# In a two-layer decoder trunk, two of the four token sums of the seven-product stage are prepared some slots later, and a weight splitter is held to one piece per slot

## The chip, the cores and the metric

The kernel runs on one core of one Trainium2 chip. The metric is the device time of one execution in microseconds (us). Before the change the median of three runs was 1451.13 us (1450.94 to 1451.14).

## What is computed

Two decoder layers on x of shape (1, 512, 1024) in float32. Layer 0 mixes tokens with dilated sliding-window attention, layer 1 with a recurrent block (RG-LRU). After either mixer comes the same gated ConvFFN, and every sub-layer is wrapped in two RMSNorms. The change sits in the ConvFFN alone, which runs once per layer:

```python
def conv_ffn(x, w_up, conv_w, conv_b, w_down):
    u = causal_dwconv(x @ w_up, conv_w, conv_b)      # w_up: 1024 x 6144, conv over 3 tokens
    g, v = u[..., :D_FF], u[..., D_FF:]              # D_FF = 3072
    return (jax.nn.gelu(g, approximate=True) * v) @ w_down

for layer in range(DEPTH):                           # DEPTH = 2
    x = x + rms_norm(mixer(rms_norm(x, ...)), ...)
    h = rms_norm(x, norm_ffn_pre[layer])
    h = conv_ffn(h, ffn_w_up[layer], ffn_conv_w[layer], ffn_conv_b[layer], ffn_w_down[layer])
    x = x + rms_norm(h, norm_ffn_post[layer])
```

## The kernel before

**Numbers in two parts.** Every float32 operand of a matmul is split into a high part (ScalarE, a copy rounded to fp32r, L153) and a low part (VectorE, the difference, L154). A product is then three matmul passes: high by high, high by low, low by high (`PASSES`). So each piece of weights also takes one ScalarE and one VectorE instruction. In the profile `whi` and `wlo` are the two parts of weights, `raw` the weights as loaded, `hT` the transposed activations (two parts), `T` the token sums, `B` their unsplit form, `ps` PSUM banks, `u` the convolved outputs.

**The queue of weight pieces.** `plan` lists the weight chunks in the order of their use. `load` (L274 on) brings a chunk into one of three `raw` buffers. `pump` (L245 on) takes the next piece of a chunk and writes its two parts into a pair of buffers. There are `HALVES = 16` such pairs, and `state["live"]` counts those in use: a piece adds one or two, `done` takes one or two off once the matmuls that read it have been written. `tick` (L303 on) runs between the parts of the program: it advances the side jobs (generators, which say after how many ticks they want to go on) and then lets `pump` split one piece when 12 (`HALVES - 4`) or more pairs are in use, two when fewer are.

**Seven products for eight.** For the FFN's column groups j = 3 to 10 (`SEVEN`) one of the two column tiles of each half of `w_up` is computed with a scheme of seven half-size products in place of eight (`seven`, `chain`). It needs sums of weight blocks, made in place in `raw` by VectorE (`across` L205, `upper` L209) and by adding DMAs on GpSimd's queue (`add_rows` L191), and sums of token blocks, made by the side job `token_sums` (L732 on): its `whole` adds the two parts of `hT` (L749), a subtraction follows (L764 to L780), and `parted` splits the sum into its home `T` (two ScalarE and two VectorE instructions). The third sum is made of `b12`, the fourth of `b21`.

**Slots.** The order of the stage is written out in slots. A cycle of 15 slots (`CYCLE`) holds one chain: its seven products stand at the slots of `AT` (`{5: 0, 1: 3, 3: 4, 2: 8, 6: 9, 7: 14, 4: 20}`, product: slot; 20 lies in the next cycle), and the slots between hold quarters of ordinary products (L340 matmuls). In the first cycle slot 5 is empty, since no chain came before. `slot` (L793 on) writes the slot's matmuls (L833 for a chain product, 12 of them), then what has come due of `later`, then calls `tick`. Of `later` three things matter here: after product 3 the `seed` (ScalarE: L843 saves one bank to `part`, L844 writes the negated bank `a` into bank `c`), after products 6 and 7 the subtractions L848 and L851, and after each finished tile the convolution (`finish`: ScalarE L679, VectorE L683 twice, then L695 or L697). Product 2 in slot 8 adds to the bank that the seed reads and product 6 in slot 9 to the one that it writes, so product 2 waits for the seed. The third token sum is read by product 7 (slot 14), the fourth by product 4 (slot 20).

Every engine works through its own instructions in the order in which they were written, so what stands ahead of the seed on ScalarE is set by which slot's `tick` wrote it. Pieces run about one cycle ahead: those that the first cycle splits are used in the second.

Of the kernel before, what the change touches and what calls it, by code (L numbers as in the profile page):

```python
# [32 lines left out]
HALVES = 16  # L33
# [45 lines left out]
def kernel(  # L79
# [38 lines left out]
    def nm(s):  # L118
        uid[0] += 1
        return f"{s}{uid[0]}"  # L120

    def gen(dt=F32, s="g"):
        return gp.tile([P, 512], dt, tag="g", name=nm(s))

    def psum(s="ps"):
        return pp.tile([P, 512], F32, tag="ps", name=nm(s))
# [25 lines left out]
    def split(hi, lo, raw):  # L152
        nc.scalar.activation(hi, raw, AF.Copy)  # L153
        nc.vector.tensor_tensor(lo, raw, hi.bitcast(F32), op=ALU.subtract)  # L154

    plan = []
    state = {"dma": 0, "cv": 0, "used": 0, "live": 0, "next": 0, "hold": False}
    raws, units, pieces = {}, {}, []
    sides, first_w, first_y, one = [], [], [], []

# [124 lines left out]
    def chunk():  # L285
        i = state["next"]
        state["next"] += 1
        return i

    def take(i, j):  # L290
        while (i, j) not in units:
            before = state["live"]
            pump(1)
            assert before != state["live"], (i, j, state)
        return units[i, j]

    def done(n=2):
        state["live"] -= n
# [4 lines left out]
    def tick():  # L303
        for s in list(sides):
            s[0] -= 1
            if s[0] <= 0:
                try:
                    s[0] = next(s[1])
                except StopIteration:
                    sides.remove(s)  # L310
        if not state["hold"]:
            pump(1 if state["live"] >= HALVES - 4 else 2)

    def drain():
        while sides:
            tick()
# [21 lines left out]
    def mm3(dst, l, r, start, stop):  # L338
        for n, (a, b) in enumerate(PASSES):
            mm(dst, l[a], r[b], start=start and n == 0, stop=stop and n == 2)  # L340
# [391 lines left out]
    def token_sums(hT, T):  # L732

        assert len(sides) == 1
        d = dp.tile([P, 4, D], F32, name=nm("x_kept"))
        nc.gpsimd.dma_start(d, X[0])
        kept.append(d)
        homes = cp.tile([P, 4, D], F32R, tag="x_sb", name=nm("T"))
        homes = [homes[:, n] for n in range(4)]
        homes += [cp.tile([P, D], F32R, tag="gain", name=nm("T"), bufs=2) for _ in range(2)]  # L740
        homes = [[h[:, 0:512], h[:, 512:1024]] for h in homes]
        homes += [[gen(F32R, "T") for _ in range(2)] for _ in range(2)]
        homes = [[h.rearrange("p (k t) -> p k t", k=2) for h in hs] for hs in homes]
        yield 1

        def both(k0, n):
            o = gen(s="B").rearrange("p (k t) -> p k t", k=2)
            hi, lo = (h[:, k0 : k0 + 2, n * 256 : n * 256 + 256] for h in hT)
            tt(o, hi.bitcast(F32), lo.bitcast(F32), op=ALU.add)  # L749
            return o  # L750

        tt = nc.vector.tensor_tensor

        def whole(k0, n):
            return [both(k0 + 2 * k, n) for k in range(2)]

        def parted(n, b):
            for k in range(2):
                split(homes[2 * n][k], homes[2 * n + 1][k], b[k])

        b11, b12 = whole(0, 0), whole(0, 1)
        yield 1
        for k in range(2):
            tt(b11[k], b11[k], b12[k], op=ALU.subtract)  # L764
        parted(0, b11)
        yield 1
        b22 = whole(4, 1)
        for k in range(2):
            tt(b12[k], b12[k], b22[k], op=ALU.subtract)
            tt(b22[k], b22[k], b11[k], op=ALU.add)  # L770
        yield 1
        parted(1, b22)
        T.extend([homes[2 * n], homes[2 * n + 1]] for n in range(4))
        yield 5
        parted(2, b12)
        yield 4
        b21 = whole(4, 0)
        yield 1
        for k in range(2):
            tt(b21[k], b21[k], b22[k], op=ALU.subtract)  # L780
        yield 1
        parted(3, b21)
# [3 lines left out]
    def seven(hT, T, begin, before):  # L786

        due = []

        def later(n, f):  # L790
            due.append([n, f])

        def slot(emit):  # L793
            emit()
            for d in list(due):
                d[0] -= 1
                if d[0] < 0:
                    due.remove(d)
                    d[1]()
            tick()  # L800

        def block(kr, n):
            return lambda h, k: hT[h][:, 4 * kr + k, n * 256 : n * 256 + 256]

        def turn(n):
            return lambda h, k: T[n][h][k // 2][:, k % 2]

        right = {
            1: block(0, 0), 2: block(1, 0), 3: block(1, 1), 5: turn(0), 6: turn(1), 7: turn(2), 4: turn(3),
        }  # L810

        def finish(b, ps, j):
            f = begin(b, ps, j)
            later(1, f)

        def chain(j, b0):
            i = chunk()
            y = {}
            t = []

            def step(n):
                name, b = LEFT[n]
                W = take(i, name)
                if b not in y:
                    y[b] = psum()
                if not t:
                    t.append(gen(s="part"))
                p5, z = t[0][:, 0:256], t[0][:, 256:512]
                a = y[0][:, 0:256] if 0 in y else None
                c = y[1][:, 0:256]  # L830
                for k in range(4):
                    for q, (wa, ha) in enumerate(PASSES):
                        mm(  # L833
                            y[b][:, 0:256], W[wa][0][:, k, :], right[n](ha, k), start=n in (1, 5) and k == q == 0,
                            stop=k == 3 and q == 2, skip_group_check=True,
                        )
                done(1)
                if n == 5:
                    later(1, lambda: nc.scalar.activation(p5, c, AF.Copy))
                elif n == 3:  # L840

                    def seed():
                        nc.scalar.activation(z, c, AF.Copy)  # L843
                        nc.scalar.activation(c, a, AF.Copy, scale=-1.0)  # L844

                    later(1, seed)
                elif n == 6:
                    later(1, lambda: nc.vector.tensor_tensor(y[0][:, 256:512], z, c, op=ALU.subtract))  # L848
                    later(2, lambda: finish(b0, y[0], j))
                elif n == 7:  # L850
                    later(1, lambda: nc.vector.tensor_tensor(y[1][:, 256:512], c, p5, op=ALU.subtract))  # L851
                elif n == 4:
                    later(1, lambda: finish(b0 + 1, y[1], j))

            return lambda n: lambda: step(n)

        def quarters(i, m, j, b):
            ps = []

            def quarter(n):  # L860
                W = take(i, m)
                if not n:
                    ps.append(psum())
                for k in (2 * n, 2 * n + 1):
                    mm3(
                        ps[0], [w[k // 4][:, k % 4, :] for w in W], [h[:, k, :] for h in hT], k == 0, k == KD - 1
                    )
                if n % 2:
                    done(1)
                if n == 3:  # L870
                    later(1, lambda: finish(b, ps[0], j))

            return [lambda n=n: quarter(n) for n in range(4)]

        steps = {}
        fill = quarters(before, 1, SEVEN[0] - 1, 3)
        for n, j in enumerate(SEVEN):
            f = chain(j, 0)
            steps.update((CYCLE * n + AT[p], f(p)) for p in AT)
            i = chunk()  # L880
            steps.update((CYCLE * n + m, q) for m, q in zip((1, 2, 6, 7, 10, 11, 12, 13), fill + quarters(i, 0, j, 2)))
            fill = quarters(i, 1, j, 3)
        after = chunk()
        end = CYCLE * len(SEVEN)
        steps[end + 3] = steps.pop(max(steps))
        fill += quarters(after, 0, SEVEN[-1] + 1, 0)
        for m in range(max(steps) + 1):
            if m in steps or m >= end:
                slot(steps[m] if m in steps else fill.pop(0))
        for f in fill:  # L890
            slot(f)
        while due:
            slot(lambda: None)
        return after

    def attention(hT, post, pre):
# [536 lines left out]
```

## Time and profile before

| what | value |
|---|---|
| median of three runs | 1451.13 us (1450.94 to 1451.14) |
| the profiled execution, own time | 1451.21 us |
| its span, first to last instruction | 1449.4 us |
| mean granted TensorE clock | 0.997 |
| VectorE busy | 970.3 us (67%) |
| ScalarE busy | 734.9 us (51%) |
| GpSimd busy | 177.6 us (12%) |

The profile shows one execution. "Busy" is the time in which an engine had an instruction in work; PE is TensorE's matmuls, PEld its weight loads, DVE is VectorE, ACT ScalarE, POOL GpSimd. A row of the timeline gives the start in us from the span's start, the duration in us of a run of like instructions, their number after the x, and in brackets how long the engine had been idle before and which instruction released it. The stage with the chains runs once in layer 0 (its first chain begins at 563.28 us) and once in layer 1 (1113.26 us).

### The profile page before, as it was taken

The numbers are of one execution on the slowest core, as the hardware profiler recorded it, in microseconds if no ns is written. First come the engines' busy times: TensorE is split into PE (matmuls) and PEld (weight loads), VectorE is DVE, ScalarE is ACT, GpSimd is POOL, SyncE is SP. The second block draws the span as 40 slices with busy tenths as digits, with TensorE's granted clock in tenths as the row PEclk, the third lists the DMA queues.
The fourth block names the chain that finished last, engine by engine and source line by source line (L and its number), as shares of the span: only waits on it lengthen the run. The fifth ranks groups of instructions, "written<-read, shape, count | busy, mean of one in ns | idle before, by whom it ended". The sixth has DMA issues, their size and how long they took to land.

```text
span 1449.4 us, 20563 instructions
## 1 busy us (share of the span) xinstructions
PE 1436.0 (99%) x7437; PEld 1232.4 (85%) x7437; DVE 970.3 (67%) x2115; ACT 734.9 (51%) x1644; POOL 177.6 (12%) x311
## 2 busy tenths in 40 slices
PE   9999999999999999999999999999999999999998
PEld 7888888888888898989988888888898899988886
DVE  6767746464646879877774348769779877764333
ACT  7656636262615555555543335589454555554231
POOL 0340514040402101101000001000100111000000
PEclk9999999999999999999999999999999999999999
DMA  7653636373736254554452322432434545453201
GB/s 225 207 147 111 168 119 200 113 211 103 199 113 208 91 180 89 140 132 105 141 203 87 115 74 88 131 116 72 133 126 124 137 107 141 124 189 116 87 1 59
DMA packets 142846, 189.66 MB, mean 131 GB/s; under 512 B 9312, under 2 KB 119352, under 8 KB 142232
## 3 DMA queue, kind: packets, MB, share of 16 engines
q1 hardware_dynamic: 114280, 145.48, 31.3%
q0 software_dynamic: 27616, 41.82, 12.1%
q8 instruction: 58, 0.95, 0.3%
q10 hardware_dynamic: 848, 1.05, 0.2%
q14 instruction: 44, 0.36, 0.1%
HBM read 168.83 MB, written 19.49 MB: 130 GB/s over the span
## 4 chain that ended last, share of the span: by engine, by line
PE 91%; ACT 4%; DVE 3%; issue 1%; DMA 0%; DVEq 0%; ACTq 0%
PE ps L340 43%; PE acc L340 24%; PE ps L833 11%; PE v L1027 8%; PE v L957 1%; DVE xb L1236 1%; DVE wlo L154 1%; PE O L1178 1%; PE S L1123 1%; ACT whi L153 1%; PE S L1077 1%; ACT sig L1257 1%; PE O L340 1%; PE tr L422 1%; ACT sig L1276 0%
## 5 line engine op out<-in xcount | busy, mean ns | idle before, releaser
L340 PE MATMUL ps<-hT,whi 128*128 128x512 f32 (+1 forms) x2240 | 645.1, 373 | 0.0
L340 PEld LDWEIGHTS ps<-hT,whi 128*128 128x128 f32 x2240 | 404.1, 189 | 68.6
L340 PE MATMUL ps<-hT,wlo 128*128 128x512 f32 (+1 forms) x1120 | 415.7, 371 | 0.0
L154 DVE TENSOR_TENSOR wlo<-raw,whi 128x512 fp32r<-128x512 f32 x408 | 269.2, 687 | 185.2 <-ACT whi L153 185.1
L153 ACT ACTIVATE whi<-raw 128x512 fp32r<-128x512 f32 x408 | 244.0, 626 | 223.5 <-PE acc L340 118.2
L340 PEld LDWEIGHTS ps<-hT,wlo 128*128 128x128 f32 x1120 | 211.0, 188 | 37.1
L340 PE MATMUL acc<-whi,ahi 128*128 128x512 f32 x512 | 199.6, 390 | 0.0
L340 PE MATMUL acc<-whi,alo 128*128 128x512 f32 x512 | 199.3, 389 | 0.1
L340 PE MATMUL acc<-wlo,ahi 128*128 128x512 f32 x512 | 199.2, 389 | 0.0
L147 ACT ACTIVATE whi<-raw,first_w 128x128 fp32r<-128x128 f32 (+1 forms) x432 | 146.9, 426 | 53.6 <-PE ps L340 30.9
L683 DVE SCALAR_TENSOR_TENSOR u<-ps,cols,u 128x511 f32<-128x511 f32 x192 | 143.6, 748 | 42.5 <-ACT u L679 39.2
L148 DVE SCALAR_TENSOR_TENSOR wlo<-raw,first_w,whi 128x128 fp32r<-128x128 f32 (+1 forms) x432 | 139.6, 390 | 1.3 <-ACT whi L147 1.3
L340 PEld LDWEIGHTS acc<-whi,alo 128*128 128x128 f32 x512 | 96.1, 188 | 20.5 <-DVE alo L154 0.5
L340 PEld LDWEIGHTS acc<-wlo,ahi 128*128 128x128 f32 x512 | 96.1, 188 | 19.8
L340 PEld LDWEIGHTS acc<-whi,ahi 128*128 128x128 f32 x512 | 96.1, 188 | 19.8
L679 ACT ACTIVATE u<-ps,cols 128x512 f32<-128x512 f32 x96 | 73.8, 769 | 69.9 <-DVE ps L848 39.7
L1027 PE MATMUL v<-whi,hT 128*128 128x512 f32 x320 | 102.3, 393 | 0.0
L833 PE MATMUL ps<-T,whi 128*128 128x256 f32 x512 | 94.9, 284 | 0.0
L191 POOL DMA_DIRECT2D raw<-in_ffn_w_up_dram x32 | 41.5, 1483 | 370.1 <-DVE wlo L154 232.2
L383 POOL DMA_DIRECT2D turned<-T x36 | 19.7, 547 | 531.4 <-DVE T L377 527.5
L390 POOL DMA_DIRECT2D ft<-turned x144 | 78.8, 555 | 40.9 <-issue 17.0
L833 PEld LDWEIGHTS ps<-T,whi 128*128 128x128 f32 x512 | 82.0, 194 | 1.6
(196 smaller groups left out, 1607.7 us busy)
## 6 DMA issues: line engine op xcount, KB each, us to landing
raw<-in_ffn_w_up_dram SPq DMA_DIRECT2D x48, 1024.0 KB
raw<-in_attn_w_qkv_dram SPq DMA_DIRECT2D x67, 512.0 KB
raw<-in_ffn_w_down_dram SPq DMA_DIRECT2D x24, 1024.0 KB
raw<-in_ffn_w_up_dram POOLq DMA_DIRECT2D x32, 256.0 KB, 4.7
raw<-in_lru_w_in_dram SPq DMA_DIRECT2D x8, 1024.0 KB
turned<-T POOLq DMA_DIRECT2D x28, 256.0 KB, 2.5
ft<-turned POOLq DMA_DIRECT2D x112, 64.0 KB, 5.8
vrows<-v SPq DMA_DIRECT2D x16, 256.0 KB
```

Source lines behind the costliest of these rows:

```text
L147: nc.scalar.activation(hi[:, k], raw[:, k], AF.Copy, scale=w)
L148: nc.vector.scalar_tensor_tensor(lo[:, k], raw[:, k], w, hi[:, k].bitcast(F32), op0=ALU.mult, op1=ALU.subtract)
L153: nc.scalar.activation(hi, raw, AF.Copy)
L154: nc.vector.tensor_tensor(lo, raw, hi.bitcast(F32), op=ALU.subtract)
L191: nc.gpsimd.dma_start(to, src, accum_op=ALU.add)
L340: mm(dst, l[a], r[b], start=start and n == 0, stop=stop and n == 2)
L383: nc.gpsimd.dma_start(d, T)
L390: nc.gpsimd.dma_start(t[32 * c : 32 * c + 32].rearrange("j (b x) -> j b x", b=4), d.rearrange("(b j) (c x) -> c j b x", j=32, c=4)[c],)
L679: nc.scalar.activation(u, ps, AF.Identity, scale=cc[:, j : j + 1], bias=cc[:, 48 + j : 49 + j])
L683: nc.vector.scalar_tensor_tensor(u[:, d:], ps[:, : S - d], wc, u[:, d:], op0=ALU.mult, op1=ALU.add)
L833: mm(y[b][:, 0:256], W[wa][0][:, k, :], right[n](ha, k), start=n in (1, 5) and k == q == 0, stop=k == 3 and q == 2, skip_group_check=True,)
L1027: mm(banks[t], hT[a][:, k, t * P : (t + 1) * P], W[b][k % 2][:, 0, :], start=(k, a, b) == (0, 0, 0), stop=(k, a, b) == (KD - 1, 1, 0),)
```

## The change

```diff
@@ state
-    state = {"dma": 0, "cv": 0, "used": 0, "live": 0, "next": 0, "hold": False}
+    state = {"dma": 0, "cv": 0, "used": 0, "live": 0, "next": 0, "hold": False, "even": False}
@@ tick
         if not state["hold"]:
-            pump(1 if state["live"] >= HALVES - 4 else 2)
+            pump(1 if state["even"] or state["live"] >= HALVES - 4 else 2)
@@ token_sums
         parted(1, b22)
         T.extend([homes[2 * n], homes[2 * n + 1]] for n in range(4))
-        yield 5
+        yield 8
         parted(2, b12)
-        yield 4
+        yield 3
         b21 = whole(4, 0)
         yield 1
         for k in range(2):
@@ seven
             fill = quarters(i, 1, j, 3)
+        state["even"] = True
         after = chunk()
...
         while due:
             slot(lambda: None)
+        state["even"] = False
         return after
```

A `yield n` means: go on n ticks later. The third sum's split (`parted(2, b12)`) is written three slots later, and with 8 + 3 for 5 + 4 ticks everything of the fourth sum two slots later. In the first cycle this moves the third split from the tick of slot 2 to that of slot 6, the fourth sum's additions (L749) from slot 7 to slot 9, its subtraction (L780) from 8 to 10, its split from 9 to 11. The flag `even` makes `tick` ask for one piece whatever `live` is.

On ScalarE, in the first cycle of layer 0, before (`T_5668` is the high part of the third sum, `whi` are weight pieces, L843 and L844 the seed, L839 the copy after product 5; of the four pieces behind the `T` rows the first reads the block that L209 changes):

```order
L839 ACTIVATE part_5948<-ps_5947 128x256
L153 ACTIVATE whi_5973<-raw_5682 128x512
L153 ACTIVATE T_5668<-B_5718 128x512
L153 ACTIVATE T_5668<-B_5720 128x512
L153 ACTIVATE whi_5989<-raw_5682 128x512
L153 ACTIVATE whi_6006<-raw_5682 128x512
L153 ACTIVATE whi_6022<-raw_5900 128x512
L153 ACTIVATE whi_6026<-raw_5900 128x512
L843 ACTIVATE part_5948<-ps_5947 128x256
L844 ACTIVATE ps_5947<-ps_5993 128x256
L153 ACTIVATE whi_6048<-raw_5682 128x512
L679 ACTIVATE u_6065<-ps_5965,cols_1279 128x512
```

The same place on ScalarE with the change (buffer numbers shift by a few):

```order
L839 ACTIVATE part_5948<-ps_5947 128x256
L153 ACTIVATE whi_5973<-raw_5682 128x512
L153 ACTIVATE whi_5985<-raw_5682 128x512
L153 ACTIVATE whi_6002<-raw_5682 128x512
L153 ACTIVATE whi_6018<-raw_5900 128x512
L153 ACTIVATE whi_6022<-raw_5900 128x512
L843 ACTIVATE part_5948<-ps_5947 128x256
L844 ACTIVATE ps_5947<-ps_5989 128x256
L153 ACTIVATE T_5668<-B_5718 128x512
L153 ACTIVATE T_5668<-B_5720 128x512
L153 ACTIVATE whi_6044<-raw_5682 128x512
L679 ACTIVATE u_6061<-ps_5965,cols_1279 128x512
```

The two `T` rows moved from ahead of four weight pieces and the seed to right behind the seed; nothing else changed place here.

On VectorE at the same place, before (`T_5669` is the low part of the third sum):

```order
L154 TENSOR_TENSOR wlo_5974<-raw_5682,whi_5973 128x512
L209 TENSOR_TENSOR raw_5682<-raw_5682 128x4x128
L154 TENSOR_TENSOR T_5669<-B_5718,T_5668 128x512
L154 TENSOR_TENSOR T_5669<-B_5720,T_5668 128x512
L154 TENSOR_TENSOR wlo_5990<-raw_5682,whi_5989 128x512
L154 TENSOR_TENSOR wlo_6007<-raw_5682,whi_6006 128x512
L154 TENSOR_TENSOR wlo_6023<-raw_5900,whi_6022 128x512
L154 TENSOR_TENSOR wlo_6027<-raw_5900,whi_6026 128x512
```

And with the change:

```order
L154 TENSOR_TENSOR wlo_5974<-raw_5682,whi_5973 128x512
L209 TENSOR_TENSOR raw_5682<-raw_5682 128x4x128
L154 TENSOR_TENSOR wlo_5986<-raw_5682,whi_5985 128x512
L154 TENSOR_TENSOR wlo_6003<-raw_5682,whi_6002 128x512
L154 TENSOR_TENSOR wlo_6019<-raw_5900,whi_6018 128x512
L154 TENSOR_TENSOR wlo_6023<-raw_5900,whi_6022 128x512
L154 TENSOR_TENSOR T_5669<-B_5718,T_5668 128x512
L154 TENSOR_TENSOR T_5669<-B_5720,T_5668 128x512
```

The `T` pair moved from right behind L209 to behind the four low parts.

On VectorE some slots on, the rows of the fourth sum before (L749 and L780 make it, `T_5672` and `T_5673` are its low part):

```order
L749 TENSOR_TENSOR B_6044<-hT_4820,hT_4821 128x512
L749 TENSOR_TENSOR B_6046<-hT_4820,hT_4821 128x512
L154 TENSOR_TENSOR wlo_6049<-raw_5682,whi_6048 128x512
L683 SCALAR_TENSOR_TENSOR u_6065<-ps_5965,cols_1275,u_6065 128x511
L683 SCALAR_TENSOR_TENSOR u_6065<-ps_5965,cols_1275,u_6065 128x510
L780 TENSOR_TENSOR B_6044<-B_6044,B_5803 128x512
L780 TENSOR_TENSOR B_6046<-B_6046,B_5805 128x512
L154 TENSOR_TENSOR wlo_6072<-raw_5682,whi_6071 128x512
L154 TENSOR_TENSOR T_5672<-B_6044,T_5670 128x512
L154 TENSOR_TENSOR T_5673<-B_6046,T_5671 128x512
L697 TENSOR_TENSOR u_5891<-u_5891,u_6065 128x512
L848 TENSOR_TENSOR ps_5993<-part_5948,ps_5947 128x256
```

And with the change, from the piece ahead of them on:

```order
L154 TENSOR_TENSOR wlo_6066<-raw_5682,whi_6065 128x512
L749 TENSOR_TENSOR B_6083<-hT_4820,hT_4821 128x512
L749 TENSOR_TENSOR B_6085<-hT_4820,hT_4821 128x512
L697 TENSOR_TENSOR u_5891<-u_5891,u_6061 128x512
L848 TENSOR_TENSOR ps_5989<-part_5948,ps_5947 128x256
L780 TENSOR_TENSOR B_6083<-B_6083,B_5803 128x512
L780 TENSOR_TENSOR B_6085<-B_6085,B_5805 128x512
L683 SCALAR_TENSOR_TENSOR u_6104<-ps_5989,cols_1275,u_6104 128x511
L683 SCALAR_TENSOR_TENSOR u_6104<-ps_5989,cols_1275,u_6104 128x510
L154 TENSOR_TENSOR T_5672<-B_6083,T_5670 128x512
L154 TENSOR_TENSOR T_5673<-B_6085,T_5671 128x512
```

The fourth sum's six instructions moved behind pieces and convolution steps that used to follow them; L848 comes ahead of its subtraction. Layer 1's first cycle shows the same three movements. On TensorE, GpSimd's queue and SyncE's queue no row changes place in either layer, and no weight piece changes place against another piece.

## The prediction

> **What bounds the kernel now.** I read the page first, then the waits of TensorE, then the stretch around the one wait that matters.
>
> ```profile
> span 1449.4 us, 20563 instructions
> PE 1436.0 (99%) x7437; PEld 1232.4 (85%) x7437; DVE 970.3 (67%) x2115; ACT 734.9 (51%) x1644; POOL 177.6 (12%) x311
> PE 91%; ACT 4%; DVE 3%; issue 1%; DMA 0%; DVEq 0%; ACTq 0%
> ```
>
> TensorE is busy for 99% of the span and carries 91% of the chain that ended last. No matmul is added or taken away, so this change can only move time through TensorE's waits. The view of the waits, for TensorE's matmuls and then its weight loads, has these:
>
> ```profile
> PE ps L833 <- ACT ps L844: 4.5, 2, 2.3
> PE warm L1352 <- DVE one L1397: 1.5, 1, 1.5
> PE v L957 <- ACT hT L442: 0.2, 1, 0.2
> PE tr L433 <- DMA x_sb<-in_x_dram: 0.2, 1, 0.2
> ...
> PEld ps L833 <- ACT ps L844: 5.4, 2, 2.7
> ```
>
> The last three matmul waits belong to the start of the program. What is left is one wait, once per layer, of a chain product (L833) for ScalarE's seed (L844): 2.3 us each by the matmuls, 2.7 us by the loads. The timeline of TensorE, ScalarE and VectorE shows it in layer 0:
>
> ```profile
> 575.48 0.50 PE L833 MATMUL ps<-hT,whi 128*128 128x256 f32 x2 [2.27 <-ACT ps L844]
> 585.44 0.40 PE L833 MATMUL ps<-T,whi 128*128 128x256 f32 x2
> 593.86 0.40 PE L833 MATMUL ps<-T,whi 128*128 128x256 f32 x2
> ...
> 568.15 0.62 ACT L153 ACTIVATE whi<-raw 128x512 fp32r<-128x512 f32 x1
> 568.67 1.14 ACT L153 ACTIVATE T<-B 128x512 fp32r<-128x512 f32 x2
> 572.57 2.19 ACT L153 ACTIVATE whi<-raw 128x512 fp32r<-128x512 f32 x4 [2.75 <-DVE raw L209]
> 574.67 0.36 ACT L843 ACTIVATE part<-ps 128x256 f32<-128x256 f32 x1
> 575.06 0.37 ACT L844 ACTIVATE ps<-ps 128x256 f32<-128x256 f32 x1
> 575.34 0.62 ACT L153 ACTIVATE whi<-raw 128x512 fp32r<-128x512 f32 x1
> 575.86 0.77 ACT L679 ACTIVATE u<-ps,cols 128x512 f32<-128x512 f32 x1
> 577.17 0.63 ACT L153 ACTIVATE whi<-raw 128x512 fp32r<-128x512 f32 x1 [0.53 <-PE ps L833]
> ...
> 571.85 0.69 DVE L209 TENSOR_TENSOR raw<-raw 128x512 f32<-128x512 f32 x1
> 572.45 1.29 DVE L154 TENSOR_TENSOR T<-B,T 128x512 fp32r<-128x512 f32 x2
> 573.66 2.49 DVE L154 TENSOR_TENSOR wlo<-raw,whi 128x512 fp32r<-128x512 f32 x4
> ```
>
> The row at 575.48 is product 2 in slot 8. 585.44 is product 7 (slot 14), the first reader of the third token sum; 593.86 is product 4 (slot 20), the first reader of the fourth. The decisive row is ScalarE's at 572.57: it had been **idle for 2.75 us**, waiting for VectorE's L209. The third sum's pair on ScalarE was over by 569.81 (568.67 + 1.14), before that idle time began. On VectorE the pair starts at 572.45, behind L209. The chain of work that ended last, in this window, says the same:
>
> ```profile
> 571.85 0.70 DVE raw L209
> ...
> 573.11 1.65 ACT whi L153 x3
> 574.76 0.28 ACT part L843
> ...
> 575.06 0.38 ACT ps L844
> ...
> 575.48 4.42 PE ps L833 x24
> ```
>
> So the wait ends by VectorE's backlog up to L209, then four pieces, then the seed. No row of a token sum is on it. Layer 1 repeats it:
>
> ```profile
> 1125.47 0.50 PE L833 MATMUL ps<-hT,whi 128*128 128x256 f32 x2 [2.28 <-ACT ps L844]
> ...
> 1118.65 1.15 ACT L153 ACTIVATE T<-B 128x512 fp32r<-128x512 f32 x2
> 1122.56 2.19 ACT L153 ACTIVATE whi<-raw 128x512 fp32r<-128x512 f32 x4 [2.75 <-DVE raw L209]
> ...
> 1121.84 0.69 DVE L209 TENSOR_TENSOR raw<-raw 128x512 f32<-128x512 f32 x1
> ```
>
> **Part 1, the flag: 0.** It could matter only in a tick of the chains that finds fewer than 12 pairs in use. Counting `live` by hand through the slots of both layers gives 13 in the tick of slot 0 and 14 to 16 in every later one: from there on a slot's `done` takes off one at most and `pump` fills up again. The limit is 1 already. The order of the instructions agrees: no weight piece changes place against another.
>
> **Part 2, the third sum's split, three slots later: 0.** It moves two ScalarE and two VectorE instructions per layer, and no DMA.
>
> On ScalarE the pair leaves 568.67 to 569.81. The next instruction there, the piece at 572.57, reads the block that L209 has just changed, so it still starts when L209 ends: 571.85 + 0.69 = 572.54. What VectorE does up to L209 has not moved and needs nothing of the pair. Hence L209, the four pieces (2.10 us to L843's start), L843 and L844 stand where they stood, and so does TensorE's wait: the removed 1.14 us was covered by the 2.75 us of idle. The pair now runs behind L844. ScalarE's pieces go at 2.10 / 4 = 0.52 us each, so the pair takes 575.34 to about 576.4, the next piece ends at about 577.0, the convolution step L679 ends at about 577.7, and the last piece starts at 577.6 instead of 577.17.
>
> On VectorE the first low part no longer queues behind the pair: it starts when its high part is there, 572.57 + 0.62 = 573.2 instead of 573.66. VectorE's like instructions go at (573.66 − 572.45) / 2 = 0.60 us, so four take until 575.6. The pair needs ScalarE's result, 575.34 + 0.62 = 576.0, and is over at about 577.3. Product 7 wants it at 585.44: **8.1 us of cover**. By 577.3 VectorE is where it was:
>
> ```profile
> 577.27 0.69 DVE L154 TENSOR_TENSOR wlo<-raw,whi 128x512 fp32r<-128x512 f32 x1
> 577.87 1.53 DVE L683 SCALAR_TENSOR_TENSOR u<-ps,cols,u 128x511 f32<-128x511 f32 x2
> ...
> 581.12 1.29 DVE L154 TENSOR_TENSOR T<-B,T 128x512 fp32r<-128x512 f32 x2
> ...
> 584.20 1.53 DVE L683 SCALAR_TENSOR_TENSOR u<-ps,cols,u 128x511 f32<-128x511 f32 x2 [0.85 <-ACT u L679]
> 585.64 1.28 DVE L154 TENSOR_TENSOR wlo<-raw,whi 128x512 fp32r<-128x512 f32 x2
> ```
>
> **Part 3, the fourth sum, two slots later: 0.** From 577.27 to 585.64 VectorE has the same instructions as before in another order, so the stretch is as long as it was but for idle time. Before, it held 0.85 us of idle, because L848, and with it ScalarE's L679, came behind the fourth sum. Now L848 comes ahead of its subtraction, and that idle goes. In exchange the first low part waited about 0.7 us (572.54 to 573.2), which is already in the 577.3 above. The fourth sum's low part comes last instead of at 581.12: it starts no earlier than 584.20 + 1.44 (the step from 584.20 to 585.64) less the vanished idle, about 584.8, and ends by about 586.0 with 1.29 us. Product 4 wants it at 593.86: **7.9 us of cover**. The pieces behind it shift from 585.64 to about 586.0, and they are of a chain that begins a cycle later still.
>
> Bounds for all of this, per layer. The gain cannot pass the pair's 1.14 us, and I exclude it, since ScalarE was idle behind the pair for longer. The loss cannot pass the pair's 1.04 us (two at 0.52) on ScalarE behind the seed, and I exclude that too as long as the 8.1 and 7.9 us hold. VectorE gets a few waits for its own earlier results that the trace does not show in these places; the nearest row, the dependent L683 pair, is 1.53 us for two and leaves no gap to see, so 0 to 0.1 us, on an engine that nobody waits for there.
>
> **The sum**, against the profiled execution's 1451.21 us (span 1449.4, the other 1.8 before and behind it): 1451.21 + 0 + 0 + 0 = 1451.2. That execution lies 0.08 above the median of the three runs, 1451.13, so I predict **1451.1 us**, no change.
>
> **What the wait is worth, for the rivals.** After each wait the clock falls for a while:
>
> ```profile
> 576.80:580.20 3.40, 3.40 (x18) 3.30 (x17) 3.37 (x6) 0.80 (x2) 0.00 (x0) 0.51 0.62 77
> 1126.40:1129.60 3.20, 3.20 (x18) 3.20 (x17) 3.17 (x6) 0.85 (x2) 0.14 (x1) 0.50 0.74 89
> ```
>
> In these windows the third number from the right is TensorE's granted clock: 0.51 over 3.40 us and 0.50 over 3.20 us, that is 1.67 and 1.60 us lost. With the waits themselves (2.27 + 2.28) the two places cost 4.55 + 3.27 = 7.8 us in all.
>
> The Trainium skill, "TensorE: Matmul & The Clock Gate", Part 1: The HAM clock gate, has the clock halve after at least one idle window of about 3.4 us and come back after one busy one, with windows that run freely. The half rate and its length agree with the rows here; the condition does not, since 2.27 us of idle (2.7 by the loads) were enough. By the page's figure a wait of 2.3 us need not cost more than itself, and the two places would be worth an estimated 4.6 us and not 7.8; the forecast is the same by either.
>
> **The rivals.**
>
> *The pair was on the path after all* (3%). Who only counts instructions sees two fewer ahead of the seed: L844 comes 1.14 us sooner and the wait shrinks to 1.1 us, in both layers 1451.1 − 2.3 = 1448.8, or less if the clock then no longer falls. For it speaks the order on ScalarE; against it the 2.75 us of idle between pair and piece.
>
> *The waits go altogether* (2%): 1451.1 − 7.8 = 1443.3. That needs L209 some 2.3 us sooner, that is other work taken from VectorE ahead of it. The change takes none.
>
> *The clock's fall is a matter of chance* (2%). If its windows are not tied to the program, one fall or both can stay out at the same waits: 1451.1 − 1.6 = 1449.5 or 1451.1 − 3.3 = 1447.8. Against it: three runs within 0.20 us, and the profiled one within 0.08 of their median.
>
> The Trainium skill, in the same Part 1 of "TensorE: Matmul & The Clock Gate", says that the windows are not reset when a program starts, which would make the fall vary from run to run; the three runs do not show that.
>
> *Slower: the third sum comes too late* (3%). Its place is product 7 in slot 14. It decides when the low part ends after 585.44, 8.1 us later than I work out, because ScalarE or VectorE behind the seed is held up by something that I have not seen. TensorE would then stop as it does now in slot 8, at the price of such a stop: 2.3 + 1.6 = 3.9 us per layer, 1451.1 + 7.8 = 1458.9. For it speaks that ScalarE's queue behind the seed grows by 1.04 us; against it the size of the gap.
>
> *The flag acts* would be a fifth: it would hold back a piece where two were split, and so shorten ScalarE's run ahead of the seed. The unmoved pieces exclude it, and I give it nothing.
>
> **How the numbers follow.** No change 90%, with a range of its own of 1450.6 to 1451.7; the four rivals 3, 2, 2 and 3%. A difference under 0.2% (2.9 us) is about what a measurement of this kernel cannot tell from no change. Faster by more than that, under 1448.2: the waits gone, half of the clock's chance, and a little of the first rival where it takes the clock's fall along, 4%. Slower, over 1454.0: the late sum, 3%. Within: 93%. The range needs only the first case for 8 in 10; I add a layer's pair on the slow side (1451.1 + 1.04) and one fall of the clock on the fast side (1451.1 − 1.7): 1449.4 to 1452.2.
>
> **What would show it.** In the profile after, product 2 still waits for L844, twice, 2.3 us each, and ScalarE is idle ahead of the four pieces for 3.8 us instead of 2.75 (from 568.15 + 0.62 to 572.57), released by L209. The `T` pair stands behind L844; the clock falls as before. No other wait of TensorE appears. I am wrong if L209 no longer starts 3.6 us ahead of product 2 (575.48 − 571.85), or if TensorE waits in slot 14 or 20.

## The result and the profile after

The changed kernel takes 1449.62 us (median of 14 runs, 1448.1 to 1451.28), the kernel before, run beside it, 1450.99 us (14 runs, 1447.95 to 1451.39). The ratio, estimated from all runs and not from the two medians, is 0.9998, with a 95% interval of 0.999 to 1.0006: no change. The runs of **both** kernels fall into the same three groups, near 1448.1, 1449.4 and 1451.1 us; the medians differ because they happen to lie in different groups (changed: 2, 6 and 6 runs; before: 2, 3 and 9).

TensorE's waits in the changed kernel, from the view of the waits (engine, line, whom it waited for: us in total, times, longest). Lines behind the first edit in `seven` (L883 of before) stand one or two further down:

```profile
PE ps L833 <- ACT ps L844: 4.6, 2, 2.3
PE warm L1354 <- DVE one L1399: 1.5, 1, 1.5
PE v L959 <- ACT whi L147: 0.3, 1, 0.3
PE v L959 <- ACT hT L442: 0.2, 1, 0.2
```

It is still the one wait, once per layer, of product 2 for the seed. The timeline of TensorE, ScalarE and VectorE at that place in layer 0 (this run stands 0.23 us earlier than the one shown of before):

```profile
575.25 0.58 PE L833 MATMUL ps<-hT,whi 128*128 128x256 f32 x2 [2.27 <-ACT ps L844]
...
572.34 2.19 ACT L153 ACTIVATE whi<-raw 128x512 fp32r<-128x512 f32 x4 [3.80 <-DVE raw L209]
574.43 0.36 ACT L843 ACTIVATE part<-ps 128x256 f32<-128x256 f32 x1
574.82 0.37 ACT L844 ACTIVATE ps<-ps 128x256 f32<-128x256 f32 x1
575.11 1.14 ACT L153 ACTIVATE T<-B 128x512 fp32r<-128x512 f32 x2
...
571.62 0.69 DVE L209 TENSOR_TENSOR raw<-raw 128x512 f32<-128x512 f32 x1
573.00 2.50 DVE L154 TENSOR_TENSOR wlo<-raw,whi 128x512 fp32r<-128x512 f32 x4 [0.70 <-ACT whi L153]
575.76 1.29 DVE L154 TENSOR_TENSOR T<-B,T 128x512 fp32r<-128x512 f32 x2 [0.27 <-ACT T L153]
581.42 0.42 DVE L848 TENSOR_TENSOR ps<-part,ps 128x256 f32<-128x256 f32 x1
581.75 1.29 DVE L780 TENSOR_TENSOR B<-B,B 128x512 f32<-128x512 f32 x2
584.40 1.28 DVE L154 TENSOR_TENSOR T<-B,T 128x512 fp32r<-128x512 f32 x2
```

The pair of the third sum has gone from ahead of the four pieces, and ScalarE's idle time there has grown from 2.75 to 3.80 us by just that much. L209 still starts 3.63 us ahead of product 2 (575.25 − 571.62; before 575.48 − 571.85 = 3.63). The wait is the same 2.27 us. One thing did move: L848 starts at 581.42 instead of 582.93, which is 1.3 us sooner in the two runs' common time. TensorE does not wait for it here (ScalarE's convolution step L679 does, after 3.47 us of idle); the experiments come back to it.

### The profile page after: what moved, and what is told of

It reads as the page before. It is cut to its first block, busy times and chain, and to the rows that moved or that the text cites. A ratio compares the mean times of both kernels' runs of the same rounds, so it can differ in the third digit from the quotient of the medians.

```text
span 1449.1 us, 20565 instructions
## 1 busy us (share of the span) xinstructions
PE 1435.5 (99%) x7437; PEld 1232.3 (85%) x7437; DVE 970.6 (67%) x2115; ACT 735.1 (51%) x1644; POOL 178.3 (12%) x311
## 4 chain that ended last, share of the span: by engine, by line
PE 91%; ACT 4%; DVE 3%; issue 1%; DVEq 0%; ACTq 0%
PE ps L340 43%; PE acc L340 24%; PE ps L833 11%; PE v L1029 8%; PE v L959 1%; DVE xb L1238 1%; DVE wlo L154 1%; PE O L1180 1%; PE S L1125 1%; ACT whi L153 1%; PE S L1079 1%; ACT sig L1259 1%; PE O L340 1%; PE tr L422 1%; ACT sig L1278 0%
## 5 line engine op out<-in xcount | busy, mean ns | idle before, releaser
L679 ACT ACTIVATE u<-ps,cols 128x512 f32<-128x512 f32 x96 | 73.8, 769 | 72.4 <-DVE ps L848 42.1
```

Of the source, the lines that this page charges most:

```text
L679: nc.scalar.activation(u, ps, AF.Identity, scale=cc[:, j : j + 1], bias=cc[:, 48 + j : 49 + j])
```

## The experiments

The theory: what ends product 2's wait is VectorE's queue up to L209, then the pieces between L209 and the seed on ScalarE. The token sums' place matters only if it moves L209, or ScalarE's work exceeds its idle time, or a product finds its operand missing. The first rival: instructions ahead of the seed cost their time wherever they stand. A second question was open: whether the three groups are falls of TensorE's clock.

### The flag alone (e6_flag)

Against the changed kernel:

```diff
-        yield 8
+        yield 5
         parted(2, b12)
-        yield 3
+        yield 4
```

> The flag alone, the token sums as before. The order of instructions is that of the kernel before, so this is that kernel again: runs near 1451.1, 1449.4 and 1448.1, ratio 1 within its interval. Were the flag to act, the four pieces ahead of the seed would be fewer and the wait shorter by 0.5 us for each.

Measured: 1449.39 us (11 runs: 1, 5 and 5 in the three groups), before beside it 1449.31 us; ratio 1.0001 (0.9992 to 1.001). The flag does nothing. Its profiled run happened to be the one of the fastest group, with a span of 1446.0 us, which bears on the second question. TensorE's wait in layer 0, and busy times and clock of the stretches behind the wait in both layers (the granted clock is the third number from the right):

```profile
575.04 0.50 PE L833 MATMUL ps<-hT,whi 128*128 128x256 f32 x2 [2.27 <-ACT ps L844]
```

```profile
575.00:578.40 3.40, 3.36 (x26) 3.32 (x27) 3.37 (x7) 1.82 (x3) 1.07 (x1) 1.00 0.75 93
1125.00:1128.40 3.40, 3.40 (x23) 3.05 (x22) 3.37 (x6) 0.98 (x2) 0.00 (x0) 1.00 0.63 77
```

The same stretches of the changed kernel, whose profiled run is of the slowest group (span 1449.1 us):

```profile
575.20:578.90 3.70, 3.65 (x18) 3.66 (x19) 3.40 (x6) 2.87 (x5) 1.09 (x1) 0.54 0.82 99
1125.20:1128.60 3.40, 3.36 (x16) 3.36 (x17) 3.10 (x6) 2.83 (x5) 0.99 (x1) 0.52 0.93 117
```

With the same wait of 2.27 us the clock stays at 1.00 in one run and falls to about one half for some 3.4 us in the other. That is 1.6 to 1.7 us per layer, close to the distance of the groups (1.3 to 1.7 us).

### TensorE kept busy in the wait (e4_fill)

Against the changed kernel:

```diff
             if m in steps or m >= end:
+                if m == 8:
+                    warm = psum("warm")
+                    for _ in range(10):
+                        mm(warm, hT[0][:, 0, 0:P], hT[0][:, 0, :], start=True, stop=True)
                 slot(steps[m] if m in steps else fill.pop(0))
```

> The changed kernel with ten needless matmuls (128x512, into a bank that nobody reads) ahead of product 2 in the first cycle of both layers, about 10 x 0.227 = 2.3 us, the length of the wait. The wait for the seed is not shortened, but TensorE is busy in it. If the runs near 1451.1, 1449.5 and 1448.1 differ by two, one and no falls of the clock, every run must now be near 1448.1 with a mean clock of 0.999 and no spread. If the spread has another cause, it stays and the median stays near 1449.6 to 1451.

Measured: 1447.88 us, all 11 runs between 1447.66 and 1448.42; ratio 0.9989 (0.998 to 0.9998). TensorE around product 2, and the windows of both layers:

```profile
572.58 2.43 PE L893 MATMUL warm<-hT 128*128 128x512 f32 x10
575.03 0.51 PE L833 MATMUL ps<-hT,whi 128*128 128x256 f32 x2
```

```profile
572.00:580.00 8.00, 7.98 (x47) 6.79 (x46) 7.00 (x12) 5.60 (x11) 2.33 (x2) 1.00 0.73 132
1122.00:1130.00 8.00, 7.99 (x47) 6.79 (x46) 7.69 (x13) 4.20 (x9) 1.27 (x1) 1.00 0.64 94
```

Product 2 starts when it did (3.64 us behind the start of L209, which here is at 571.39), the clock does not fall, and the spread is gone. So the three groups are two, one and no falls: shown.

### The third sum one slot earlier (e1_early)

Against the kernel before:

```diff
-        yield 5
+        yield 4
         parted(2, b12)
-        yield 4
+        yield 5
```

> The kernel before, with the third sum's split one slot EARLIER (4 and 5 ticks for 5 and 4; the fourth sum stays). On VectorE the pair now stands ahead of L209. My theory (the wait ends by VectorE's queue up to L209): L209 starts 1.2 us later (two at 0.60), so does the seed, and TensorE's wait grows from 2.3 to about 3.5 us in both layers: 2.4 us slower than the runs of before that have two falls of the clock, about 1453.5, and both falls in every run. The rival (the pair counts by its place on ScalarE): ScalarE does it in its idle time as before, so nothing changes, 1451.1.

Measured: 1453.91 us (7 runs, 1452.97 to 1454.31), ratio 1.0029 (1.0017 to 1.004). TensorE, ScalarE and VectorE in layer 0:

```profile
576.23 0.79 PE L833 MATMUL ps<-hT,whi 128*128 128x256 f32 x2 [3.48 <-ACT ps L844]
```

```profile
573.33 2.19 ACT L153 ACTIVATE whi<-raw 128x512 fp32r<-128x512 f32 x4 [3.95 <-DVE raw L209]
```

```profile
570.80 1.29 DVE L154 TENSOR_TENSOR T<-B,T 128x512 fp32r<-128x512 f32 x2
572.00 0.68 DVE L154 TENSOR_TENSOR wlo<-raw,whi 128x512 fp32r<-128x512 f32 x1
572.61 0.69 DVE L209 TENSOR_TENSOR raw<-raw 128x512 f32<-128x512 f32 x1
```

The pair stands ahead of L209, and the wait has grown by 1.21 us, the two VectorE instructions. On ScalarE the pair still stands ahead of the seed, and again idle time follows it (3.95 us). So VectorE's order up to L209 sets the wait, and one slot in that direction costs where three in the other gave nothing. Of the time, 2.4 us are the two longer waits (1447.9 without falls becomes 1450.3); I put the other 3.6 us down to falls of the clock; the trace has one in either layer, and the one in layer 0 lasted longer than those shown so far (window, then the clock third from the right):

```profile
576.20:582.20 6.00, 5.97 (x26) 5.87 (x27) 5.96 (x11) 3.06 (x5) 0.00 (x0) 0.50 0.48 58
```

### More work on ScalarE behind the pair (e2_act2, e2_act8)

Against the kernel before:

```diff
         parted(2, b12)
+        junk = gen(s="junk").rearrange("p (k t) -> p k t", k=2)
+        for _ in range(2):                  # 8 in e2_act8
+            nc.scalar.activation(junk, b12[0], AF.Copy)
```

> The kernel before with two needless copies (128x512, output unused) written on ScalarE right behind the third sum's pair. My theory: they take 2 x 0.52 us of the 2.75 us for which ScalarE waits for L209, so TensorE's wait stays 2.3 us and the time stays with the kernel before (runs near 1451.1, 1449.4 and 1448.1). The rival (instructions ahead of the seed on ScalarE cost their time): wait 3.3 us, 2.1 us slower, about 1453.2.

Measured: 1449.27 us (11 runs: 2, 6 and 3 in the groups), ratio 0.9997 (0.9989 to 1.0006). TensorE and ScalarE in layer 0 (lines are three further down):

```profile
575.10 0.80 PE L836 MATMUL ps<-hT,whi 128*128 128x256 f32 x2 [2.28 <-ACT ps L847]
```

```profile
572.19 2.19 ACT L153 ACTIVATE whi<-raw 128x512 fp32r<-128x512 f32 x4 [1.57 <-DVE raw L209]
```

The idle time shrinks from 2.75 to 1.57 us and the wait stays: two more instructions ahead of the seed are free. This profiled run is of the middle group, and in it the clock (third number from the right) falls behind the wait of layer 0 and not behind that of layer 1:

```profile
575.10:578.50 3.40, 3.40 (x16) 3.40 (x17) 3.37 (x7) 1.78 (x3) 1.03 (x1) 0.50 0.80 99
1125.10:1128.50 3.40, 3.40 (x27) 3.31 (x28) 3.37 (x7) 1.77 (x3) 1.03 (x1) 1.00 0.94 117
```

> The same with eight needless copies. 8 x 0.52 = 4.2 us is more than the 2.75 us of idle by 1.4 us. My theory: only the excess counts, TensorE's wait becomes about 3.7 us in both layers, 2.8 us slower than the kernel before's runs with two falls of the clock, about 1453.9, with both falls in every run. The rival (all of it counts): wait 6.5 us, 8.4 us slower, about 1459.5.

Measured: 1457.11 us (5 runs, 1455.41 to 1457.56), ratio 1.0049 (1.0036 to 1.0061). ScalarE and then TensorE in layer 0:

```profile
569.20 5.27 ACT L778 ACTIVATE junk<-B 128x512 f32<-128x512 f32 x8
574.38 2.17 ACT L153 ACTIVATE whi<-raw 128x512 fp32r<-128x512 f32 x4
```

```profile
577.27 0.51 PE L836 MATMUL ps<-hT,whi 128*128 128x256 f32 x2 [4.58 <-ACT ps L847]
```

The kind of effect was right, its size was not: the copies took 5.27 / 8 = 0.66 us each and not 0.52. (Unlike the pieces they all write one tile, and unrounded float32; which of the two makes them longer, no run shows.) So the four pieces start at 574.38 instead of at L209's end (572.03 in this run), 2.3 us late, and the wait is 2.27 + 2.3 = 4.6 us. Only what exceeds the idle time counts. The two waits make 1447.9 into 1452.5; I put the remaining 2.9 to 5.1 us down to falls of the clock. In the profiled run the one in layer 0 lasted 3.4 us; the one in layer 1 was longer, with TensorE's clock at 0.52 on average over 6.70 us, in part of which TensorE was idle:

```profile
1127.30:1134.00 6.70, 4.45 (x21) 4.45 (x22) 6.66 (x11) 4.32 (x9) 1.02 (x1) 0.52 0.49 61
```

### The third sum as late as it can be (e5_late)

Against the changed kernel:

```diff
-        yield 8
+        yield 15
         parted(2, b12)
-        yield 3
+        yield 1
```

> The changed kernel with the third sum's split as late as the order allows, in the tick of slot 13 right ahead of product 7 (15 ticks in place of 8), the fourth sum's parts behind it in the ticks of slots 14 to 16. My theory: with the token sums gone from VectorE's queue ahead of it, L848 and the convolution behind it come some 2 us sooner, the pair ends at about 584.9 us against product 7's 585.4, so no wait in slot 14 or at most some tenths, and the time stays with the changed kernel (1448.1, 1449.5 or 1451.1 by run). The slower rival of the prediction, brought to its point: a wait in slot 14 of 2 us or more, 1453 and over.

Measured: 1450.88 us (11 runs, 1449.6 to 1452.56), ratio 1.0008 (0.9999 to 1.0017), with groups near 1449.65, 1451.0 and 1452.6, some 1.8 us above those of the kernel before beside it (1447.76, 1449.2 and 1450.7). The wait for the seed is there as ever; the new one is this:

```profile
PE ps L833 <- DVE T L154: 1.0, 2, 0.6
...
594.24 0.39 PE L833 MATMUL ps<-T,whi 128*128 128x256 f32 x1 [0.61 <-DVE T L154]
```

It does not stand in slot 14 but in slot 20: the fourth sum, pushed behind the third, comes too late for product 4. The expectation had looked at the third alone. By TensorE's matmuls these waits are 1.0 us for both layers, by its weight loads 1.7. Seven slots more than the change cost some 1.8 us; the change itself is far from this edge.

### The cause taken away: pieces held behind the seed (e3_hold, e8_hold4)

Against the changed kernel:

```diff
             if m in steps or m >= end:
+                state["hold"] = m in (2, 3, 4)      # (4,) in e8_hold4
                 slot(steps[m] if m in steps else fill.pop(0))
```

> The changed kernel with the pieces of slots 2, 3 and 4 of the first cycle held back until the seed is written (no piece is split in those three ticks; the later slots go on with one each). The seed then stands on ScalarE right behind a piece that needs nothing of L209. My theory: it runs as soon as product 3 is done, product 2 waits for nothing, the clock never falls there, and the time is 1448.1 minus 4.55 us of waits, about 1443.5, without a spread. If pieces are then too late for a later product, TensorE waits there instead and part of the gain is gone. The rival (the wait is for something other than the seed's place in the queue): no change, 1448 to 1451.

Measured: **1442.85 us**, all 5 runs within 1442.78 to 1442.91; ratio 0.9955 (0.9942 to 0.9967). TensorE's waits, then ScalarE:

```profile
PE warm L1355 <- DVE one L1400: 1.5, 1, 1.5
PE v L960 <- ACT whi L147: 0.2, 1, 0.2
PE v L960 <- ACT hT L442: 0.2, 1, 0.2
```

```profile
567.75 0.62 ACT L153 ACTIVATE whi<-raw 128x512 fp32r<-128x512 f32 x1
570.10 0.38 ACT L843 ACTIVATE part<-ps 128x256 f32<-128x256 f32 x1 [1.73 <-PE ps L833]
570.51 0.37 ACT L844 ACTIVATE ps<-ps 128x256 f32<-128x256 f32 x1
```

The seed now waits for product 3 and for nothing else, and the stage has no wait left. Against the runs without falls (1447.9, as in e4_fill) this is 5.1 us, 2.5 per layer: a little more than the 2.27 us of idle that TensorE's row shows, close to the 2.7 of its weight loads.

> The changed kernel with only the two pieces of slot 4 held back until the seed is written. The seed still stands behind two pieces that wait for L209, but two pieces of 0.52 us fewer. My theory: the wait shrinks by 1.04 us to about 1.2 us in both layers; without a fall of the clock 1448.1 minus 2.1, about 1446.0. What is open is the clock: if an idle of 1.2 us cannot make it fall, all runs are near 1446.0; if it can, there is a second group of runs 1.6 us higher.

Measured: 1445.68 us, all 7 runs within 1445.53 to 1445.72; ratio 0.9971 (0.9959 to 0.9982). The wait is 1.23 us, as worked out:

```profile
574.05 0.50 PE L833 MATMUL ps<-hT,whi 128*128 128x256 f32 x2 [1.23 <-ACT ps L844]
```

In the profiled run the clock does not fall behind it, and the seven runs lie within 0.2 us with a mean clock of 0.999 or more.

### The same without the change (e7_hold_alone), and with either half of it (e9_hold_fourth, e10_hold_third)

The hold as in e3_hold, with these ticks ahead of the third sum's split and ahead of the fourth sum: 5 and 4 as before (e7_hold_alone), 5 and 6 (e9_hold_fourth), 8 and 1 (e10_hold_third). None has the flag.

```diff
-        yield 5
+        yield 5                             # 8 in e10_hold_third
         parted(2, b12)
-        yield 4
+        yield 6                             # 4 in e7_hold_alone, 1 in e10_hold_third
```

> The hold of e3_hold in the kernel before, without the change: the third sum's pair stands ahead of the seed on ScalarE again (slot 2), the fourth sum's parts in slots 7 to 9. My theory: the pair (1.1 us, over at about 569.6) is done before product 3, so the seed waits for nothing but TensorE, and the time is that of e3_hold, 1442.9, without a spread. The rival (the change is worth something once the wait is gone): slower than e3_hold, by up to 2.1 us, 1445.

Measured: 1445.78 us, 6 runs within 1445.59 to 1445.86; ratio 0.997 (0.9958 to 0.9981). The rival held, and my theory of this run fell: with the wait gone the change is worth 2.9 us (1445.78 − 1442.85). TensorE and VectorE of e7_hold_alone:

```profile
582.43 0.50 PE L833 MATMUL ps<-T,whi 128*128 128x256 f32 x2 [1.26 <-DVE ps L848]
```

```profile
577.14 1.29 DVE L780 TENSOR_TENSOR B<-B,B 128x512 f32<-128x512 f32 x2
...
579.54 1.29 DVE L154 TENSOR_TENSOR T<-B,T 128x512 fp32r<-128x512 f32 x2
...
581.95 0.42 DVE L848 TENSOR_TENSOR ps<-part,ps 128x256 f32<-128x256 f32 x1
```

Product 7 in slot 14 adds to a bank that L848 has yet to read. L848 stands on VectorE behind the whole fourth sum. With product 2 no longer late, product 7 could start some 2.3 us sooner (at 582.43 − 1.26 = 581.17, against 583.46 in the profiled run of e6_flag) and now waits for L848, 1.26 us per layer. For both layers the waits are 2.5 us by the matmuls and 3.4 by the weight loads, around the 2.9 us of the time.

> The hold of e3_hold, and of the change the fourth sum's shift alone (its parts two slots later; the third sum's split stays in slot 2; no flag). In e7_hold_alone product 7 waits 1.3 us per layer for L848, which VectorE reaches only behind the fourth sum's additions, subtraction and split. My new theory: the fourth sum's shift alone brings L848 ahead of the subtraction and the split, that wait goes, and the time is e3_hold's, 1442.9. The rival (the third sum's shift does it): 1445.8 as in e7_hold_alone.

Measured: 1442.8 us (5 runs, 1442.75 to 1442.84), ratio 0.9946 (0.9934 to 0.9959). VectorE there:

```profile
579.50 0.42 DVE L848 TENSOR_TENSOR ps<-part,ps 128x256 f32<-128x256 f32 x1
579.83 1.29 DVE L780 TENSOR_TENSOR B<-B,B 128x512 f32<-128x512 f32 x2
...
583.08 1.28 DVE L154 TENSOR_TENSOR T<-B,T 128x512 fp32r<-128x512 f32 x2
```

> The hold of e3_hold, and of the change the third sum's shift alone (split in slot 6; the fourth sum stays in slots 7 to 9; no flag). My theory: L848 still stands behind the whole fourth sum on VectorE, product 7 waits about 1.3 us per layer, 1445.8 as in e7_hold_alone. The rival: 1442.9 as in e3_hold.

Measured: 1445.89 us (6 runs, 1445.85 to 1446.0), ratio 0.9968 (0.9955 to 0.998), with product 7 waiting 1.35 us for L848. So the fourth sum's two slots bring L848 forward by 2.45 us (581.95 to 579.50) and are the half that counts. The third sum's three slots are worth nothing with or without them. Neither half was run alone without the hold.

## Why the prediction was right, and where it was not

**The flag, 0:** right, by the run of the flag alone.

**The third sum, 0:** right, and for the reason given: ScalarE's idle time covered the pair. The rows after agree to the hundredths (idle 3.80 us worked out as 3.8, VectorE's first low part 0.7 us late, the pair over by 577.05 against 577.3 worked out in a run 0.23 us later). That L209 is the gate is shown by e1_early, that the place on ScalarE is not by e2_act2 and e2_act8.

**The fourth sum, 0:** right for this kernel, but the working stopped too early. I saw that L848 comes sooner and booked it as idle time gone on VectorE. I didn't ask what reads behind L848: product 7, which had only 2.1 us of room behind it in the run shown (585.44 − 582.93 − 0.42), and 0.6 in the run of e6_flag without falls:

```profile
582.48 0.42 DVE L848 TENSOR_TENSOR ps<-part,ps 128x256 f32<-128x256 f32 x1
...
583.46 0.40 PE L833 MATMUL ps<-T,whi 128*128 128x256 f32 x2
```

So the change did move something near the path. Its gain, 2.9 us for both layers once that wait is gone, lies hidden behind the wait for the seed that it leaves in place.

**The clock's fall as a matter of chance (2%):** this step failed. The falls do come and go at the same waits, in both kernels, and three runs and a profiled one that agree were too thin to exclude it. The median after, 1449.62, lies where I put one fall out (1449.5), and outside the 1450.6 to 1451.7 that I gave the likeliest case; the wider range held it, by the margin of one fall that I had added. That is in part luck: the group without falls, 1448.1, lies outside the wider range too. The groups are where the prices put them: 1451.1 − 1.6 and − 3.3. The Trainium skill, "TensorE: Matmul & The Clock Gate", Part 1: The HAM clock gate, has windows that run freely, and a clock that halves after at least one idle window of about 3.4 us. The runs agree with the first, since falls come and go at unchanged waits, and not with the second: 2.27 us of idle made the clock fall in some runs. An idle of 1.23 us never did in 7 runs.

**The price of the wait, 4.55 us plus the falls:** a little low. Taking it away gave 5.1 us below the runs without falls.

## What to carry to other kernels

An instruction in front of a late one is on the path only if the engine would otherwise have worked there: read the idle time and its releaser just ahead of the late instruction before counting what its queue holds. A change behind a wait can be worth something and show nothing, until that wait is gone; for a reordering, follow also the instructions that come *sooner*, and look who reads behind them. Here holding three slots' weight pieces back, with the fourth sum moved, beats both kernels: 1442.8 us against about 1450.8 for the kernel before beside it.

## What the hardware showed that I had not expected

The same program with the same waits takes one of three times, 1448, 1449.4 or 1451 us, as TensorE's clock falls to one half after none, one or both of two idle times of 2.27 us; each fall lasted about 3.4 us there and cost about 1.6 us; behind waits of 3.5 and 4.6 us some falls lasted 3.4 us and some twice that (6.0 us at 0.50 are shown above). Filling the idle time with needless matmuls took the spread away and 1.4 us off the median beside it (1447.88 against 1449.28), though the product behind them started no sooner.

What decides whether a wait costs a fall can be read from the same traces, though no run was made to test it. The falls lie on a grid of 3.413 us that is not tied to the waits: in e2_act8 product 2 starts at 577.27 and 1129.55, which is 552.28 us apart, but the falls begin at 578.03 and 1127.57, 549.55 us or 161 steps apart, just as in the profiled runs of before (576.86 and 1126.40) and of the changed kernel (575.52 and 1125.07). Each fall lasts one or two steps of the grid. Counted from a fall of the same run, this is TensorE's idle time (by the matmuls) in the steps that come nearest to the limit, and one well above it:

| run, layer | TensorE waits (us) | step of the grid (us) | idle in the step (us) | clock behind it |
|---|---|---|---|---|
| changed, 0 | 572.98 to 575.25 | 572.11 to 575.52 | 2.27 | 0.50 |
| before, 0 | 573.21 to 575.48 | 573.44 to 576.86 | 2.04 | 0.50 |
| e5_late, 0 | 572.84 to 575.12 | 571.42 to 574.84 | 2.00 | 0.50 |
| e2_act8, 0 | 572.69 to 577.27 | 571.20 to 574.61 | 1.92 | 1.00 |
| e2_act2, 1 | 1122.80 to 1125.08 | 1121.25 to 1124.67 | 1.87 | 1.00 |

The profiles show ten falls at waits for the seed. In the step ahead of each of them TensorE was idle for 2.00 us or more, and behind no step with 1.92 us or less did the clock fall from full. As far as these profiles go, then, a wait of 2.27 us costs a fall or not by where the grid cuts it, which differs from one execution to the next, and one of 1.23 us stays below the limit wherever it is cut.
